# The opening stage of a DiT trunk kernel on one NeuronCore: vectors spread by diagonal tiles, paired squares, five parts of modulation rows between the products, and three tile pairs instead of four

## The chip, the core and the metric

The kernel runs on one core of one Trainium2 chip. The core has TensorE (PE in the profile; PEld is its weight load), VectorE (DVE), ScalarE (ACT), GpSimd (POOL) and SyncE (SP), which issues most of the DMA transfers. The metric is device time in microseconds (us) for one execution; lower is better.

## The reference, cut to what matters

The model is two layers over 256 latent tokens and 256 context tokens of width 1024, all in float32. Every sub-layer starts with an RMS norm whose gain and shift come from a modulation vector, and the first sub-layer is a half-step SwiGLU:

```python
silu_c, silu_cc = jax.nn.silu(c), jax.nn.silu(c_ctx)
m  = (silu_c  @ w_mod[0] + b_mod[0])        # 9 vectors of 1024: shift, scale, gate, ...
mc = (silu_cc @ w_mod[0] + b_mod[0])
h  = rms_norm(x, g) * (1 + scale) + shift   # for x with m, for ctx with mc
a, b = jnp.split(h @ w13, 2, axis=-1)       # w13: 1024 x 5632
x  = x + 0.5 * gate * ((jax.nn.silu(a) * b) @ w2)
```

The change touches what happens before and during the first products `h @ w13`: the norm's sum of squares, the first two of the nine modulation vectors (shift and scale of 1024 entries, for both streams), and the first tiles of `h @ w13`.

## The kernel before, in words

Activations lie transposed: `X` holds 8 parts of 128 features by 512 tokens (256 latent, then 256 context). A "part" k is one such block of 128 features, and is also one block of the contraction of `h @ w13`. Nearly every product is made three times with single-pass float32 operands (`mm3`, lines 147 to 150): each operand is split into a rounded high piece and the rest (`split`, lines 152 to 154: a cast on ACT, a subtraction on DVE), and low times high, high times high and high times low are summed in PSUM. Products that go to PE as plain float32 are two instructions each in the trace.

The program's scheduler orders the instructions of each engine by its own estimates, keeping dependencies; `tc.keep_in_program_order` (called `pin`) puts one instruction behind the instruction that was written just before it for the same engine. PSUM has 8 banks, handed out by `bank()`.

The stage to be changed is `start()` (lines 639 to 743). It loads the two vectors (`cT`), spreads silu of them over all partitions with 16 small products against the identity (line 665) into `cc`, squares the 8 parts of `X` on ACT and sums them over partitions with 8 products against `ones` (lines 679 and 680), and turns that into `rb`, the reciprocal root (lines 681 and 685). The modulation of 5 of the 8 parts comes from DVE: `use_mod` (line 80) multiplies a 128 x 1024 block of `w_mod` with `cc` and sums each row, four instructions for a part (shift and scale, two streams). The modulation of the other three parts (`NR = 3`) comes from PE: `by_rows` (lines 691 to 709) multiplies `cT` with rows of `w_mod`, copies the result to SBUF and transposes it back with small products (line 704). `finish_mod` (lines 84 to 101) adds the bias and forms the gain `gs`; it is two small DVE instructions.

Then a loop runs over the parts in `order`. Per part: load a block of weights for the first four tile pairs of `w13` (`get_raw`, line 645), split it, normalise (`xr`, line 721, DVE; then the modulation, line 724, ACT), split the result into `AH` and `AL`, and make the part's products into the eight PSUM banks `pss`. A tile pair is 128 columns of a and of b, so a part has 4 x 2 x 3 = 24 products with 512 columns. `ffn` (called with `started`) finds the first four tile pairs done and goes on with tile pair 4; each later tile pair is 48 such products.

Of the kernel before, what the change touches and what calls it, by code (L numbers as in the profile page):

```python
# [9 lines left out]
F32 = mybir.dt.float32  # L10
F32R = mybir.dt.float32r
# [11 lines left out]
NH = NF // 2  # L23
EPS = 1e-6
NMOD = 72
NR = 3
WINDOWS = (2, 4, 8, 16)
ATTN_SCALE = 0.125

# [6 lines left out]
def trunk(ctx: ExitStack, tc: tile.TileContext, I, out):  # L36
# [47 lines left out]
    def finish_mod(layer, j, n=1, ks=slice(0, NK)):  # L84
# [7 lines left out]
        V.tensor_tensor(out=m, in0=m, in1=b.broadcast_to([P, ns, n, nk]), op=ALU.add)  # L92
        sub, kind = (j + n - 1) // 3, (j + n - 1) % 3
        last = m[:, :, n - 1]
        if kind == 1:
            g0 = C_NG + (layer * 3 + sub) * NK
            g = par[:, g0 + ks.start:g0 + ks.stop].unsqueeze(1).broadcast_to([P, ns, nk])
            V.scalar_tensor_tensor(out=gs[:, st, sub, ks], in0=last, scalar=1.0, in1=g,
                                   op0=ALU.add, op1=ALU.mult)
        if kind == 2:  # L100
            V.tensor_scalar(gate[:, st, sub, ks], last, 1.0 if j == 5 else 0.5, None, ALU.mult)
# [535 lines left out]


    def start():
        ng = 4  # L640
        order = (0, 5, 1, 6, 2, 7, 3, 4)
        with tc.tile_pool(name="start", bufs=1) as sp:
            def get_raw(k):
                raw = sp.tile([P, ng, 2 * P], F32, name="raw4", bufs=2)
# [4 lines left out]
            cT = sp.tile([P, 2, NK], F32, name="cT")  # L649
            nc.sync.dma_start(out=cT, in_=I["cT"])  # L650
            nc.sync.dma_start(out=ident, in_=I["ident"])
            wm = {(0, 0): load_mod(0, 0, nc.sync)}
            for k in range(0, NK, 2):
                nc.sync.dma_start(out=X[:, k:k + 2], in_=I["xc"][:, k:k + 2])
            wm[0, 1] = load_mod(0, 1, nc.sync)
            S.activation(out=cT, in_=cT, func=AF.Silu)

            S.activation(out=rb[:, 0:1], in_=cT[:, 0, 0:1], func=AF.Sqrt, scale=0.0, bias=epsb)

            for st in range(2):  # L660
                for h in range(2):
                    ps = bank()
                    for k4 in range(4):
                        k = 4 * h + k4
                        PE.matmul(ps[:, k4 * P:k4 * P + P], cT[:, st, k:k + 1].broadcast_to([P, P]),  # L665
                                  ident, start=True, stop=True)
                    S.copy(cc[:, st, h * 512:h * 512 + 512], ps)  # L667
            nc.sync.dma_start(out=par, in_=I["par"])
            wn = [wpool.tile([P, 2, 2 * NR * P], F32, name=n, bufs=3 if i > 1 else 2)
                  for i, n in enumerate(("raw", "raw", "whi", "wlo"))]  # L670
            for i in range(4):
                nc.sync.dma_start(out=wn[i], in_=I["w_modr"][:, 2 * i:2 * i + 2])
            raws = {0: get_raw(0)}
            wm.update({(1, h): load_mod(0, 2 + h, nc.sync) for h in range(2)})
            raws[order[1]] = get_raw(order[1])
            ps = bank()
            for k in range(NK):
                sq = tmp.tile([P, 2 * T], F32, name="sq", bufs=2)
                S.activation(out=sq, in_=X[:, k], func=AF.Square)
                PE.matmul(ps, ones, sq, start=k == 0, stop=k == NK - 1)  # L680
            S.activation(out=rb, in_=ps, func=AF.Sqrt, scale=1.0 / D, bias=epsb)
            for h in range(2):
                use_mod(0, h, wm[0, h])
            finish_mod(0, 0, 2, slice(0, 1))
            V.reciprocal(rb, rb)
            sh = sp.tile([P, NK, ng - 2, 2 * P], F32R, name="sh")
            sl = sp.tile([P, NK, ng - 2, 2 * P], F32R, name="sl")
            wh, wl = ([wpool.tile([P, NK, 2 * P], F32R, name=n, bufs=3) for _ in range(2)]
                      for n in ("whi", "wlo"))

            def by_rows():

                row = sp.tile([2, 2 * NR * P], F32, name="row")
                ps = [bank() for _ in range(2)]
                for k in range(NK):
                    for j in range(2):
                        PE.matmul(ps[j][0:2, :NR * P], cT[:, :, k],  # L697
                                  wn[k // 2][:, k % 2, j * NR * P:(j + 1) * NR * P],
                                  start=k == 0, stop=k == NK - 1)
                for j in range(2):  # L700
                    S.copy(row[:, j * NR * P:(j + 1) * NR * P], ps[j][0:2, :NR * P])
                ps = bank()
                for i in range(2 * NR):
                    PE.matmul(ps[:, 2 * i:2 * i + 2], row[:, i * P:i * P + P], ident[0:2, 0:2],
                              start=True, stop=True)
                for st in range(2):
                    V.tensor_copy(mod[:, st, :16].rearrange("p (j k) -> p j k", j=2)[:, :, NK - NR:],
                                  ps[:, 0:4 * NR].rearrange("p (j k s) -> p s j k", j=2, k=NR)[:, st])
                finish_mod(0, 0, 2, slice(NK - NR, NK))

            by_rows()
            pss = [[bank(), bank()] for _ in range(ng)]
            nxt = 1
            for i, k in enumerate(order):
                raw = raws.get(k) or get_raw(k)
                split(sh[:, k], sl[:, k], raw[:, :2])
                split(wh[0][:, k], wl[0][:, k], raw[:, 2])
                split(wh[1][:, k], wl[1][:, k], raw[:, 3])
                xr = tmp.tile([P, 2 * T], F32, name="sa", bufs=2)
                h = tmp.tile([P, 2 * T], F32, name="h32", bufs=2)  # L720
                V.tensor_tensor(out=xr, in0=X[:, k], in1=rb, op=ALU.mult)
                for st in range(2):
                    ts = slice(st * T, st * T + T)
                    S.activation(out=h[:, ts], in_=xr[:, ts], func=AF.Identity,
                                 scale=gs[:, st, 0, k:k + 1], bias=mod[:, st, k:k + 1])
                if nxt < NK - NR and i in (0, 2, 4, 5):
                    for j in range(2):
                        use_mod(0, 2 * nxt + j, wm.get((nxt, j)) or
                                load_mod(0, 2 * nxt + j, nc.sync), tc.keep_in_program_order)
                    finish_mod(0, 0, 2, slice(nxt, nxt + 1))  # L730
                    nxt += 1
                split(AH[:, k, :2 * T], AL[:, k, :2 * T], h)

                def products(f, k, first, last):
                    for ab in range(2):
                        cs = slice(ab * P, ab * P + P)
                        w = (sh[:, k, f, cs], sl[:, k, f, cs]) if f < 2 else \
                            (wh[f - 2][:, k, cs], wl[f - 2][:, k, cs])
                        mm3(pss[f][ab], *w, AH[:, k, :2 * T], AL[:, k, :2 * T], first, last)

                for f in range(ng):
                    products(f, k, i == 0, i == NK - 1)
        return pss


# [14 lines left out]
def _pack(x, c, ctx, c_ctx, w_mod, b_mod, norm_g, ffn_w13, ffn_w2, w_in_a, qk_norm_g, pool_w,  # L760
# [5 lines left out]
    r["cT"] = ac(np.stack([c[0], c_ctx]).reshape(2, NK, P).transpose(2, 0, 1))  # L766
    r["w_modr"] = ac(w_mod[0][:, :2 * D].reshape(NK, P, 2, NK, P)[:, :, :, NK - NR:]
                     .transpose(1, 0, 2, 3, 4)).reshape(P, NK, 2 * NR * P)
# [70 lines left out]
```

## Time and profile before

| | |
|---|---|
| three runs, median (lowest to highest) | 1141.87 us (1141.83 to 1142.08) |
| the profiled execution | 1142.17 us, of which 1140.4 us are its span |
| TensorE's granted clock, mean | 1.000 |
| HBM read | 240.44 MB, 212 GB/s over the span |
| DVE / ACT busy, share of the span | 76% / 46% |

The span runs from the first to the last instruction. The page lists each engine's busy time, the chain of work that ended last, and groups of instructions by source line; the trace can be asked for any stretch. Matmuls are pipelined, so the duration of one includes its way through the array; what a stream of them costs is the distance from one start to the next (the pitch).

### The profile page before, as it was taken

What the parts mean: (1) busy time and instruction counts of PE and PEld (TensorE: products, weight loads), DVE (VectorE), ACT (ScalarE), POOL (GpSimd) and SP (SyncE); (2) the same over time, 40 slices, a digit from 0 to 9 for tenths busy, and PEclk for the clock granted to TensorE, in tenths of its full rate; (3) what the DMA queues carried; (4) which work ended last, traced back from release to release, by engine and by line L of the source; (5) the groups of instructions that cost most, each with busy time, mean ns of one, the idle gap of its engine ahead of it and who ended that gap; (6) DMA issues with size and microseconds to landing.
All of it is one profiled execution on the core that took longest, in us unless ns stands there. A gap on an engine that the chain in (4) does not pass through costs nothing.

```text
span 1140.4 us, 19165 instructions
## 1 busy us (share of the span) xinstructions
PE 1132.2 (99%) x7696; PEld 1033.9 (91%) x7696; DVE 863.6 (76%) x1582; ACT 522.0 (46%) x816; POOL 68.4 (6%) x140
## 2 busy tenths in 40 slices
PE   8999999999999999999999999999999999999998
PEld 4888888888888897899999999999999899999998
DVE  5967787878789979777778887656667788756663
ACT  5552212223223357664335456435445866434442
POOL 0000111122222200000000000000000000000000
PEclk9999999999999999999999999999999999999999
DMA  8844656788888850556687566456447536546543
GB/s 323 310 148 156 197 186 234 279 282 325 294 297 306 305 196 11 222 172 223 212 305 264 187 219 218 161 167 219 174 143 257 185 114 219 176 154 237 178 143 114
DMA packets 52408, 242.72 MB, mean 213 GB/s; under 512 B 5600, under 2 KB 11488, under 8 KB 38880
## 3 DMA queue, kind: packets, MB, share of 16 engines
q1 hardware_dynamic: 33888, 174.39, 43.4%
q0 software_dynamic: 18432, 67.12, 17.4%
q8 instruction: 60, 0.98, 0.4%
q14 instruction: 28, 0.23, 0.1%
HBM read 240.44 MB, written 1.05 MB: 212 GB/s over the span
## 4 chain that ended last, share of the span: by engine, by line
PE 97%; DVE 1%; ACT 1%; DMA 1%; issue 0%; SPq 0%; DVEq 0%; ACTq 0%
PE ps L148 30%; PE ps L149 30%; PE ps L150 30%; PE ps L697 1%; PE ps L618 1%; PE ps L619 1%; PE ps L617 1%; PE ps L680 1%; PE ps L665 1%; DMA raw<-in_w_out_a 0%; ACT whi L153 0%; PE ps L501 0%; PE ps L469 0%; DVE st L473 0%; PE ps L172 0%; ACT pe L477 0%
## 5 line engine op out<-in xcount | busy, mean ns | idle before, releaser
L148 PE MATMUL ps<-AH,wlo 128*128 128x258 f32 (+2 forms) x1664 | 507.1, 305 | 0.3 <-ACT AH L153 0.3
L149 PE MATMUL ps<-AH,whi 128*128 128x258 f32 (+2 forms) x1664 | 506.6, 305 | 0.0
L150 PE MATMUL ps<-AL,whi 128*128 128x258 f32 (+2 forms) x1664 | 505.5, 305 | 0.0
L153 ACT CAST whi<-raw 128x1024 fp32r<-128x1024 f32 (+2 forms) x354 | 313.7, 921 | 363.7 <-PE ps L150 260.3
L154 DVE TENSOR_TENSOR wlo<-raw,whi 128x1024 fp32r<-128x1024 f32 (+2 forms) x354 | 367.6, 1064 | 54.4 <-ACT whi L153 53.4
L148 PEld LDWEIGHTS ps<-AH,wlo 128*128 128x128 f32 x1664 | 316.3, 190 | 16.1 <-issue 1.1
L149 PEld LDWEIGHTS ps<-AH,whi 128*128 128x128 f32 x1664 | 314.3, 189 | 14.7 <-issue 0.5
L150 PEld LDWEIGHTS ps<-AL,whi 128*128 128x128 f32 x1664 | 313.4, 189 | 14.5 <-issue 0.2
L150 PE MATMUL ps<-HL,whi 128*128 128x256 f32 (+1 forms) x704 | 218.0, 310 | 0.0
L149 PE MATMUL ps<-HH,whi 128*128 128x256 f32 (+1 forms) x704 | 218.0, 310 | 0.0
L148 PE MATMUL ps<-HH,wlo 128*128 128x256 f32 (+1 forms) x704 | 218.0, 310 | 0.0
L80 DVE CUSTOM_DVE_ANT_0 wm<-wm,cc 128x1024 f32<-128x1024 f32 x138 | 164.7, 1219 | 6.1 <-DMA wm<-in_w_mod 5.0
L148 PEld LDWEIGHTS ps<-HH,wlo 128*128 128x128 f32 x704 | 132.5, 188 | 7.8
L150 PEld LDWEIGHTS ps<-HL,whi 128*128 128x128 f32 x704 | 132.5, 188 | 7.7
L149 PEld LDWEIGHTS ps<-HH,whi 128*128 128x128 f32 x704 | 132.6, 188 | 7.7
L72 POOL DMA_DIRECT2D wm<-in_w_mod x128 | 67.7, 529 | 546.2 <-DVE mod L80 508.6
L206 ACT ACTIVATE sa<-sa,cb 128x256 f32<-128x256 f32 x66 | 33.6, 510 | 119.7 <-DVE sa L205 116.4
L246 DVE SCALAR_TENSOR_TENSOR X<-ps,gate,X 128x256 f32<-128x256 f32 x64 | 30.9, 482 | 48.0 <-PE ps L150 47.9
L204 DVE COPY cb<-ps 128x1 f32<-128x1 f32 x66 | 10.3, 155 | 72.8 <-PE ps L150 72.7
L212 DVE TENSOR_TENSOR h<-ps,sa 128x512 f32<-128x512 f32 x22 | 15.2, 692 | 43.4 <-PE ps L150 34.2
L80 DVE CUSTOM_DVE_ANT_0 junk<-wm,cc 128x1024 bf16<-128x1024 f32 x34 | 41.4, 1218 | 8.6 <-ACT cc L667 7.2
L154 DVE TENSOR_TENSOR HL<-h,HH 128x256 fp32r<-128x256 f32 (+1 forms) x88 | 42.3, 485 | 0.0
(162 smaller groups left out, 705.3 us busy)
## 6 DMA issues: line engine op xcount, KB each, us to landing
raw<-in_w SPq DMA_DIRECT2D x84, 1024.0 KB, 4.9
wm<-in_w_mod POOLq DMA_DIRECT2D x128, 512.0 KB, 5.0
raw<-in_w SPq DMA_DIRECT2D x64, 704.0 KB, 4.1
wm<-in_w_mod SPq DMA_DIRECT2D x10, 512.0 KB, 6.4
raw<-in_w_in_a SPq DMA_DIRECT2D x5, 1024.0 KB, 7.8
raw<-in_w SPq DMA_DIRECT2D x8, 512.0 KB, 5.3
raw<-in_w_out_a SPq DMA_DIRECT2D x4, 1024.0 KB, 5.0
raw<-in_w_in_cu SPq DMA_DIRECT2D x4, 1024.0 KB, 4.8
```

The lines of the kernel that those rows point to most:

```text
L72: eng.dma_start(out=w, in_=I["w_mod"][layer, i])
L80: pin(V.tensor_tensor_reduce(out=res, in0=w, in1=cc[:, st, :], scale=1.0, scalar=0.0, op0=ALU.mult, op1=ALU.add, accum_out=mod[:, 2 * laye ...
L148: PE.matmul(ps, wl, xh, start=first, stop=False)
L149: PE.matmul(ps, wh, xh, start=False, stop=False)
L150: PE.matmul(ps, wh, xl, start=False, stop=last)
L153: S.copy(hi, src)
L154: pin(V.tensor_tensor(out=lo, in0=src, in1=hi.bitcast(F32), op=ALU.subtract))
L206: S.activation(out=sa[:, :T], in_=sa[:, :T], func=AF.Silu, bias=cb[:, 0:1])
L212: V.tensor_tensor(out=h32[:, :n], in0=ps[1][:, :n], in1=sa[:, :n], op=ALU.mult)
L246: V.scalar_tensor_tensor(out=X[:, m, :T], in0=ps[:, :T], scalar=gate[:, 2 * layer, sub, m:m + 1], in1=X[:, m, :T], op0=ALU.mult, op1=ALU.add)
L617: PE.matmul(ps[b], AL[:, k, ts], hi[:, ws], start=(k == 0), stop=False)
L618: PE.matmul(ps[b], AH[:, k, ts], hi[:, ws], start=False, stop=False)
```

## The change

- `order` is now (3, 4, 0, 5, 1, 6, 2, 7). The modulation of five parts, `ROWS = (3, 4, 5, 6, 7)`, comes from `by_rows`, one part at a time; that of parts 0, 1 and 2 from `use_mod` on DVE, in the loop passes 1, 2 and 4 (`jobs`).
- `by_rows(k)` makes 8 products with 32 columns of weights (`c32`, two vectors padded with zeros) and 256 columns of data, into the four 32-row quarters of one bank in turn, copies the bank to SBUF, and sums the quarters in two small products with a selecting matrix `sel`. Part 3 is done before the loop, part 4 between the halves of part 3's products, and parts 5, 6 and 7 after the first third of the products of the part before.
- `cc` is made by two DVE products of the identity with the vectors (`diag`) and four products with `ones`; the copy to SBUF moves from ACT to DVE.
- The squares of parts 0 to 5 are added in pairs on DVE, so 5 products with `ones` are left of 8.
- `rb` is finished in two halves, latent and context. The first part's products are made in two halves too.
- Four products of `ones` with a piece of `X`, whose result isn't used, stand ahead of the loop.
- Three tile pairs instead of four are made in the opening (`ng = 3`); the fourth is made in `ffn`.
- The loads are put in another order; `raw4` has four buffers.

```diff
+ROWS = (3, 4, 5, 6, 7)
...
-        V.tensor_tensor(out=m, in0=m, in1=b.broadcast_to([P, ns, n, nk]), op=ALU.add)
+        V.tensor_tensor(out=m, in0=m if src is None else src, in1=b.broadcast_to([P, ns, n, nk]),
+                        op=ALU.add)
...
-        ng = 4
-        order = (0, 5, 1, 6, 2, 7, 3, 4)
+        ng = 3
+        order = (3, 4, 0, 5, 1, 6, 2, 7)
+
+        jobs = {1: 0, 2: 1, 4: 2}
...
+            for ks in (slice(0, 2), slice(2, 4), slice(4, 6), slice(6, 7), slice(7, 8)):
+                nc.sync.dma_start(out=X[:, ks], in_=I["xc"][:, ks])
+            nc.sync.dma_start(out=par, in_=I["par"])
+            rows, raws, wm = {}, {}, {}
+            rows[3] = get_rows(3)
+            raws[3] = get_raw(3)
+            rows[4] = get_rows(4)
+            raws[4] = get_raw(4)
+            wm.update({(0, j): load_mod(0, j, nc.sync) for j in range(2)})
+            raws[0] = get_raw(0)
+            rows[5] = get_rows(5, "whi", 3)
+            raws[5] = get_raw(5)
+            wm.update({(1, j): load_mod(0, 2 + j, nc.sync) for j in range(2)})
...
+            diag = cc.rearrange("p s (k c) -> p s k c", k=NK)
+            bc = [bank() for _ in range(4)]
             for st in range(2):
+                V.tensor_tensor(out=diag[:, st], in0=ident.unsqueeze(1).broadcast_to([P, NK, P]),
+                                in1=c32[:, :, st:st + 1].broadcast_to([P, NK, P]), op=ALU.mult)
                 for h in range(2):
-                        PE.matmul(ps[:, k4 * P:k4 * P + P], cT[:, st, k:k + 1].broadcast_to([P, P]),
-                                  ident, start=True, stop=True)
-                    S.copy(cc[:, st, h * 512:h * 512 + 512], ps)
+                    PE.matmul(bc[2 * st + h], ones, diag[:, st, 4 * h:4 * h + 4],
+                              start=True, stop=True)
...
                 S.activation(out=sq, in_=X[:, k], func=AF.Square)
-                PE.matmul(ps, ones, sq, start=k == 0, stop=k == NK - 1)
-            S.activation(out=rb, in_=ps, func=AF.Sqrt, scale=1.0 / D, bias=epsb)
+                if k in (0, 2, 4):
+                    even = sq
+                    continue
+                if k < 6:
+                    V.tensor_tensor(out=sq, in0=even, in1=sq, op=ALU.add)
+                PE.matmul(ps, ones, sq, start=k == 1, stop=k == NK - 1)
+            pin = tc.keep_in_program_order
+            for b in range(4):
+                pin(V.tensor_copy(cc[:, b // 2, b % 2 * 512:b % 2 * 512 + 512], bc[b]))
...
+            def by_rows(k):
+                w = rows.pop(k)
+                for kt in range(NK):
+                    g = kt % 4
+                    pin(PE.matmul(rw[32 * g:32 * g + 32, :2 * P], c32[:, kt], w[:, kt],
+                                  start=kt < 4, stop=kt >= 4))
+                row = sp.tile([P, 2 * P], F32, name="row", bufs=2)
+                pin(S.copy(row, rw[:, :2 * P]))
                 for j in range(2):
+                    PE.matmul(rw[:, 2 * P + 2 * j:2 * P + 2 * j + 2], row[:, j * P:j * P + P], sel,
+                              start=True, stop=True)
+                finish_mod(0, 0, 2, slice(k, k + 1),
+                           rw[:, 2 * P:2 * P + 4].rearrange("p (j s) -> p s j", j=2).unsqueeze(3))
...
+            by_rows(order[0])
+            for _ in range(4):
+                pin(PE.matmul(rw[:, :2 * P], ones, X[:, 0, :2 * P], start=True, stop=True))
             for i, k in enumerate(order):
...
+                if i == 0:
+                    for ts in halves:
+                        if ts.start:
+                            pin(V.reciprocal(rb[:, ts], rb[:, ts]))
+                            subs(pin)
+                            rest(halves[0])
+                        pin(V.tensor_tensor(out=xr[:, ts], in0=X[:, k, ts], in1=rb[:, ts],
+                                            op=ALU.mult))
+                        if ts.start == 0:
+                            casts(pin)
+                        normed(ts, AH[:, k, ts])
+                        normed(ts, h[:, ts])
+                    rest(halves[1])
+                else:
+                    casts(pin)
+                    subs(pin)
+                    V.tensor_tensor(out=xr, in0=X[:, k], in1=rb, op=ALU.mult)
+                    for ts in halves:
+                        normed(ts, h[:, ts])
+                    split(AH[:, k, :2 * T], AL[:, k, :2 * T], h)
...
+                if i in jobs:
+                    d = jobs[i]
                     for j in range(2):
+                        use_mod(0, 2 * d + j, wm.pop((d, j)), tc.keep_in_program_order)
+                    finish_mod(0, 0, 2, slice(d, d + 1))
...
+                if i == 0:
+                    for ts in halves:
+                        if ts.start:
+                            by_rows(ahead)
+                        for j, (a, x) in enumerate(((0, AH), (0, AL), (1, AH))):
+                            for f, ab in ws:
+                                PE.matmul(pss[f][ab][:, ts], ws[f, ab][a], x[:, k, ts],
+                                          start=j == 0 and ts.start == 0, stop=False)
+                else:
+                    for f, ab in ws:
+                        if ahead is not None and (f, ab) == (1, 0):
+                            by_rows(ahead)
+                        mm3(pss[f][ab], *ws[f, ab], AH[:, k, :2 * T], AL[:, k, :2 * T], False,
+                            i == NK - 1)
```

Here `casts` and `subs` are the two casts (ACT) and two subtractions (DVE) that split the part's weights, `normed` is the modulation (line 724 before), `rest` the subtraction that gives `AL`, and `ahead` the next part in `order` if it is one of `ROWS`.

More of the change, by code (lines that the diff above doesn't have):

```diff
@@ L647, in get_raw, with get_rows @@
                 return raw
-            cT = sp.tile([P, 2, NK], F32, name="cT")
-            nc.sync.dma_start(out=cT, in_=I["cT"])
-            nc.sync.dma_start(out=ident, in_=I["ident"])
[L652 to L658, printed above, removed]
+            def get_rows(k, home="raw", bufs=2):
+                w = wpool.tile([P, NK, 2 * P], F32, name=home, bufs=bufs)
+                nc.sync.dma_start(out=w, in_=I["w_modr"][ROWS.index(k)])
+                return w
@@ L688, in start @@
[L688 to L699, printed above, removed]
+                if k in (0, 2, 4):
+                    even = sq
+                    continue
@@ new lines, in start @@
+                if k < 6:
[4 more added lines that the diff above has]
+                pin(V.tensor_copy(cc[:, b // 2, b % 2 * 512:b % 2 * 512 + 512], bc[b]))
+            for st in range(2):
+                ts = slice(st * T, st * T + T)
+                S.activation(out=rb[:, ts], in_=ps[:, ts], func=AF.Sqrt, scale=1.0 / D, bias=epsb)
@@ new lines, in start @@
+            rw = bank()
+            halves = [slice(st * T, st * T + T) for st in range(2)]
+            pin(V.reciprocal(rb[:, :T], rb[:, :T]))
+            def by_rows(k):
[6 more added lines that the diff above has]
+                pin(S.copy(row, rw[:, :2 * P]))
@@ L732, in start @@
-                split(AH[:, k, :2 * T], AL[:, k, :2 * T], h)
-                def products(f, k, first, last):
-                    for ab in range(2):
[L736 to L742, printed above, removed]
+                parts = ((sh[:, k], sl[:, k], raw[:, :2]), (wh[:, k], wl[:, k], raw[:, 2]))
@@ new lines, in casts, with subs, normed @@
+                def casts(pin=lambda ins: ins):
+                    for w, l, r in parts:
+                        pin(S.copy(w, r))
+                def subs(pin=lambda ins: ins):
+                    for w, l, r in parts:
+                        pin(V.tensor_tensor(out=l, in0=r, in1=w.bitcast(F32), op=ALU.subtract))
+                def normed(ts, out):
+                    st = ts.start // T
+                    S.activation(out=out, in_=xr[:, ts], func=AF.Identity,
+                                 scale=gs[:, st, 0, k:k + 1], bias=mod[:, st, k:k + 1])
```

84 lines of the change are left out of this document (38 added, 46 removed).

## The prediction

> **What bounds the kernel now.** The page comes first: busy shares, then the chain that ended last.
>
> ```profile
> span 1140.4 us, 19165 instructions
> PE 1132.2 (99%) x7696; PEld 1033.9 (91%) x7696; DVE 863.6 (76%) x1582; ACT 522.0 (46%) x816; POOL 68.4 (6%) x140
> PE 97%; DVE 1%; ACT 1%; DMA 1%; issue 0%; SPq 0%; DVEq 0%; ACTq 0%
> ```
>
> PE is busy for all but 8.2 us, and 97% of the chain is PE. So the kernel ends when PE's queue has been worked off: whatever moves the moment at which the opening's products are done moves the end by as much, and nothing later takes it up. The chain over the first 30 us shows what PE does ahead of them (start, length, line), and the timeline shows the product stream.
>
> ```profile
> 3.31 6.15 PE ps L665 x32
> 9.46 7.26 PE ps L680 x16
> 16.72 10.41 PE ps L697 x32
> 27.13 0.76 PE ps L704 x6
> 28.78 0.76 PE ps L704 x6
> 29.53 0.43 PE ps L148
> 70.08 0.39 PE L149 MATMUL ps<-AH,sh 128*128 128x512 f32 x1
> 81.88 0.39 PE L149 MATMUL ps<-AH,whi 128*128 128x512 f32 x1
> 68.66 0.60 ACT L211 ACTIVATE sa<-ps 128x512 f32<-128x512 f32 x1 [4.03 <-PE ps L150]
> ```
>
> The two L149 rows are 51 products apart: 11.80 / 51 = 0.2314 us for a product of 512 columns without a break. ScalarE's row marks the end of the first tile (three products) of the last part: its last product started a product's length (0.39) before 68.6, and the next 21 follow at 0.2314, so the 192 opening products (8 parts x 24) are off PE's queue at 73.3. They alone cost 192 x 0.2314 = 44.4. So **28.9 us of the opening is not products**, and the chain shows it gap-free: 6.15 spreading vectors, 7.26 squares, 10.41 rows, some 2 transposes, and 3.3 for the first loads.
>
> The other engines, by windows (PE, PEld, DVE, ACT busy in each):
>
> ```profile
> 0.00:5.00 5.00, 1.69 (x8) 1.72 (x9) 0.22 (x2) 3.08 (x4) 0.20 (x4) 1.00 0.50 158
> 5.00:10.00 5.00, 5.00 (x28) 4.69 (x28) 1.23 (x2) 3.29 (x6) 0.00 (x0) 1.00 0.97 356
> 30.00:35.00 5.00, 5.00 (x23) 4.05 (x22) 5.00 (x14) 3.22 (x8) 0.00 (x0) 1.00 0.60 212
> 65.00:70.00 5.00, 5.00 (x23) 4.10 (x22) 0.62 (x2) 0.60 (x1) 0.00 (x0) 1.00 0.62 210
> ```
>
> From 30 us DVE is as full as PE, and only at 65 is it ahead. Its work is hidden because a part has 24 products (5.6 us). With three tile pairs a part has 18 x 0.2314 = 4.17 us of cover.
>
> **The change, part by part.** After the change 144 products lie in the opening and 48 are tile pair 3, done at once behind it, so the same 44.4 us of products end at: start S of the first product + 44.4 + other PE work behind S + PE's gaps behind S. That is set against 73.3.
>
> *Spreading and squares.*
>
> ```profile
> 2.67 0.22 ACT L656 ACTIVATE cT<-cT 128x16 f32<-128x16 f32 x1 [0.65 <-DMA cT<-in_cT]
> L665 PE MATMUL ps<-ident,cT x6: 421/421/421, 5.8 to 6.9; 128*128 128x128 f32 x6
> L665 PE MATMUL ps<-ident,cT x7: 274/275/275, 8.3 to 9.0; 128*128 128x128 f32 x7
> L679 ACT ACTIVATE sq<-X 128x512 f32<-128x512 f32 x8 | 4.9, 628 | 2.3 <-PE ps L680 1.7 <-DMA X<-in_xc 0.6
> L163 DVE TENSOR_TENSOR acc<-acc,sq 128x512 f32<-128x512 f32 x7 | 4.8, 685 | 0.0
> L667 ACT COPY cc<-ps 128x512 f32<-128x512 f32 x4 | 2.3, 581 | 1.6 <-PE ps L665 1.6
> 45.17 1.22 DVE L80 CUSTOM_DVE_ANT_0 junk<-wm,cc 128x1024 bf16<-128x1024 f32 x1
> 46.92 1.22 DVE L80 CUSTOM_DVE_ANT_0 wm<-wm,cc 128x1024 f32<-128x1024 f32 x1
> 48.06 1.22 DVE L80 CUSTOM_DVE_ANT_0 junk<-wm,cc 128x1024 bf16<-128x1024 f32 x1
> ```
>
> The silu ends at 2.9. The diagonal product (128 x 1024 on DVE) isn't in the trace; between one 512-column add (0.69) and two (1.37) I take the 1.22 of the like-sized L80: the two halves are ready at 4.4 and 5.6. The four spreads are eight 512-column instructions; L680's pitch is 7.26 / 16 = 0.454. But PE's first 4.5 us run at half speed although the granted clock reads 1.00: L665's starts are 0.22 apart at 5.8 to 6.9 and 0.117 at 8.3 to 9.0. So 4.4 to 8.9 gives 4.9 instructions at 0.91 and the other 3.1 take 1.4: 10.3 us, against 9.46 now. Nothing is gained; the wide products only do in one piece what 32 short ones did.
>
> The five square products then stand in a chain, because `sq` has two buffers: the second square of a pair (0.63) waits for the product that reads its buffer, the add (0.69) follows, and then the product (0.91): 2.23 per pair. First product 10.3 to 11.2 (its inputs are there by 7.5), then 13.4, 15.65, and the last single one 0.63 + 0.91 later: 17.2, against 16.72 now. If spreads and squares ran without cold clock and waits, 18 x 0.454 from 4.4 would end at 12.6: that is the low end of this term, 4.6 less. The four copies of `cc` (0.58 on ACT, L667) move to DVE behind the last add (14.7) and are through by 17.2, ahead of the root.
>
> *Part 3's modulation.* It is pinned behind the last square product.
>
> ```profile
> 448.81 1.73 PE L501 MATMUL ps<-pt,VV 128*64 128x256 f32 x13 [0.37 <-ACT pt L493]
> 442.09 0.59 PE L450 MATMUL ps<-pd,poolw 128*128 128x256 f32 x2
> 27.06 0.82 PE L704 MATMUL ps<-ident,row 2*128 2x2 f32 x6
> L504 ACT COPY hn<-ps 128x256 f32<-128x256 f32 x4 | 1.5, 382 | 1.3 <-PE ps L377 1.3
> 15.27 0.17 DVE L92 TENSOR_TENSOR mod<-mod,par 128x4 f32<-128x4 f32 x1
> 15.47 0.16 DVE L98 SCALAR_TENSOR_TENSOR gs<-mod,par 128x2 f32<-128x2 f32 x1
> L174 DVE RECIPROCAL rb<-rb 128x256 f32<-128x256 f32 x4 | 7.0, 1754 | 2.2 <-ACT rb L173 2.2
> L173 ACT ACTIVATE rb<-ps,epsb 128x256 f32<-128x256 f32 x4 | 1.9, 476 | 1.3 <-PE ps L172 1.2
> L192 DVE TENSOR_TENSOR hn<-X,rb 128x256 f32<-128x256 f32 x8 | 3.0, 418 | 0.0
> L724 ACT ACTIVATE h<-sa,mod,gs 128x256 f32<-128x256 f32 x16 | 8.9, 595 | 9.4 <-DVE sa L721 6.8 <-DVE gs L98 2.4
> L153 ACT CAST AH<-h 128x512 fp32r<-128x512 f32 x8 | 5.0, 620 | 0.2
> ```
>
> The eight products are 16 instructions of 256 columns. Untiled ones stand 0.59 - 0.38 = 0.21 apart (L450); those with 64-column tiles, alternating between two, (1.73 - 0.38) / 12 = 0.1125 (L501). Four tiles in turn could reach half of that again, 0.056, if they really run four abreast. But each float32 product is two instructions for the same tile, and if the second waits for the first and all start in order, only neighbours overlap: 0.1125. I take that, the nearest row: 1.8 us; ends 0.9 and 3.4. [...]
>
> So: rows 17.2 to 19.0, copy 0.38, four transposes 3 x 0.115 + 0.25 = 0.6 (L704's pitch and length), gain 0.4, the half norm 0.42 (pinned behind the gain), modulation 0.60: **S = 21.4**. Root and half reciprocal (0.48 + 1.75 from 17.2) are done at 19.4, hidden; so are the loads: 2.2 MB of X and vectors plus 1.05 MB of rows and par lie ahead, and the windows have moved 2.6 MB by 10 us and 356 GB/s after. Later loads are further ahead still: the issues that SP gains stand behind transfers needed after 21, and POOL's loads of `w_mod` only follow freed buffers. The four idle products (1.7 us) fill the wait for DVE and are hidden.
>
> *The parts*, each from the start of its products; a gap is idle PE.
>
> ```profile
> L154 DVE TENSOR_TENSOR sl<-raw,sh 128x512 fp32r<-128x512 f32 x8 | 5.5, 685 | 0.0
> L154 DVE TENSOR_TENSOR wlo<-raw,whi 128x256 fp32r<-128x256 f32 x16 | 6.3, 418 | 0.0
> L721 DVE TENSOR_TENSOR sa<-X,rb 128x512 f32<-128x512 f32 x8 | 5.4, 686 | 0.6 <-ACT h L724 0.6
> ```
>
> Part 3: 6 products of half width (6 x 0.116 = 0.7), then `AL` is needed, but DVE has pinned ahead of it the second reciprocal (1.75), two subtractions (0.69 + 0.42) and then `rest` (0.42): a gap of 2.0. Twelve more (1.4), rows of part 4 (1.8), second half with transposes (2.6): S + 8.5. Part 4's `AH` comes 3.5 after its rows (0.38 + 0.6 + 0.4, two modulations 1.19, cast 0.62, hand-overs 0.3): S + 9.4, a gap of 0.9.
>
> Part 4 to part 0: part 0 gets its gain from `use_mod`, and the first of these is pinned behind the subtraction that gives part 4's `AL`. Two in a row start 1.14 apart (46.92, 48.06). From part 4's `AH`: 0.69 + 4.6 + gain 0.4 + modulation 1.1 + cast 0.62 = 7.4, against 4.17 of products: **a gap of 3.2**.
>
> Part 0 to part 5: products, rows and transposes take 4.17 + 1.8 + 0.46 = 6.4. DVE has four `use_mod` again; the gain of part 5 is ready 4.2 into it, just as the fourth starts (4.1). Behind that one the next `AH` is at 7.8, ahead of it at 6.4; the rows of 45 to 48 us show that the order does put other work between two L80. I take the middle: 0.7. Part 1 to part 6 is the same: 0.7. Parts 5 and 6 have no such work (0.69 `AL`, 1.1 subtractions, 0.69 norm, 1.1 modulation and 0.62 cast are 4.2, against 4.17): 0. Part 2 to part 7: the gain comes 6.7 in, against 6.4: 0.3.
>
> **Sum:** 21.4 + 44.4 + four times (1.8 + 0.46) = 9.0 + gaps 2.0 + 0.9 + 3.2 + 0.7 + 0.7 + 0.3 = 7.8, together 82.6. Against 73.3 that is 9.3 later. The profiled execution took 1142.17, 0.3 above the median shown; so 1142.17 + 9.3 = 1151.5, and by the median 1151.2. PE's work itself shrinks by only some 2.5 us, while an opening without gaps gets some 14 us in which PE waits.
>
> **Rivals.**
>
> *Four tiles abreast*: rows take 0.9. That is 0.9 less in S, part 3 and part 2, and 0.6 less in parts 0 and 1, where DVE then bounds: 3.9 less, 1147.3. For it: L501's tiles do overlap. Against: the pairs. With the low end of the squares' term as well, 1143.
>
> *PE stays the bound* (the other side): the order fills every gap, as it does now. PE's own work is 4.4 + 5.9 + 4.5 + 2.3 + 1.7 idle products + 44.4 + 9.0 = 72.2: 1140.8, no change; with four abreast, five times 0.9 less: 1136.3, faster. It decides once gaps and chains cost under some 3 us. For it: 99% busy now. Against: the pins, which put `use_mod` behind `AL`.
>
> *The clock falls back* in a gap: PE's opening shows half speed for 4.5 us, so each such gap costs 2.2 more: 1153.4, or 1155.6 for two. [...] The gap of 3.2 is the longest in the sum.
>
> *No overlap at all*, so that the change doesn't do what it says: rows take 3.4, five times 1.6 more: 1159.2.
>
> **How the numbers follow.** Forecast 0.52, four abreast 0.20, PE stays the bound 0.13, clock 0.10, no overlap 0.05. A measurement of this kernel tells about 0.2% (2.3 us) from no change. Faster by more: 0.09, from PE staying the bound with four abreast. Within: 0.04 from the same rival with pairs, and 0.05 from four abreast with early squares: 0.09. Slower: the rest, 0.82. The range reaches from four abreast with early squares (1143) to two cold gaps and a little more (1157), and leaves out 0.18.
>
> **What would show it.** The first `AH` product near 21 us; the last square product near 17; rows' starts 0.11 apart (0.06 for four abreast, 0.21 for none); a PE gap of some 3 us ahead of the second part after part 3, ended by ScalarE's cast, with four L80 on DVE before it; tile pair 3 done near 82.6. I would be wrong if the squares are through by 13, if L80 runs ahead of part 4's `AL`, or if loads come last anywhere.

## The result, and the profile after

| | before | after |
|---|---|---|
| median of 4 runs (lowest to highest) | 1141.97 us (1141.83 to 1142.39) | 1155.14 us (1154.33 to 1156.58) |
| profiled execution, and its span | 1142.17 us, 1140.4 us | 1154.33 us, 1152.6 us |
| granted TensorE clock, mean | 1.000 | 0.997 |

The changed kernel is slower: ratio 1.0116, 95% interval 1.0099 to 1.0134. That is 13.2 us by the medians and 12.2 us between the two profiled executions, where 9.3 us had been forecast. First the page: span, busy shares and the chain that ended last.

```profile
span 1152.6 us, 19270 instructions
PE 1131.5 (98%) x7748; PEld 1033.1 (90%) x7748; DVE 863.7 (75%) x1575; ACT 520.4 (45%) x811; POOL 68.4 (6%) x140
PE 93%; DVE 3%; ACT 2%; DMA 1%; issue 0%; DVEq 0%; ACTq 0%
```

TensorE has almost the same work as before (1131.5 us against 1132.2), but there are now 21.1 us of the span in which it does nothing, against 8.2. The chain says the same: PE lost 4 points, and DVE (1% to 3%) and ACT (1% to 2%) gained. Where does it end? The same ScalarE instruction of tile pair 4 (the silu, line 211 before, 213 after) in the two timelines:

```profile
79.12 0.60 ACT L211 ACTIVATE sa<-ps 128x512 f32<-128x512 f32 x1 [0.83 <-PE ps L150]
```

```profile
91.41 0.60 ACT L213 ACTIVATE sa<-ps 128x512 f32<-128x512 f32 x1 [3.10 <-PE ps L152]
```

It comes 12.3 us later, and the span is 12.2 us longer. So everything happens in the opening, and nothing later gives any of it back. Now PE's timeline of the changed kernel (start, length, line, count; in brackets the idle time before it and what ended it):

```profile
10.53 1.02 PE L699 MATMUL ps<-sq,ones 128*128 128x512 f32 x2
12.99 1.12 PE L699 MATMUL ps<-sq,ones 128*128 128x512 f32 x2 [1.44 <-DVE sq L698]
15.56 4.46 PE L699 MATMUL ps<-sq,ones 128*128 128x512 f32 x6 [1.45 <-DVE sq L698]
19.96 1.07 PE L716 MATMUL ps<-raw,c 128*32 128x256 f32 x16
21.52 0.61 PE L721 MATMUL ps<-cs,row 128*128 128x2 f32 x4 [0.49 <-ACT row L719]
22.44 1.99 PE L733 MATMUL ps<-X,ones 128*128 128x256 f32 x8 [0.31 <-DVE mod L93]
24.08 0.82 PE L810 MATMUL ps<-AH,sh 128*128 128x256 f32 x4
25.84 0.74 PE L810 MATMUL ps<-AL,sh 128*128 128x256 f32 x4 [0.70 <-DVE AL L755]
31.92 0.50 PE L150 MATMUL ps<-AH,sl 128*128 128x512 f32 x1 [0.56 <-ACT AH L155]
39.65 0.79 PE L150 MATMUL ps<-AH,sl 128*128 128x512 f32 x1 [3.30 <-ACT AH L155]
48.73 0.50 PE L150 MATMUL ps<-AH,sl 128*128 128x512 f32 x1 [1.64 <-ACT AH L155]
```

The first three rows are the chain of the squares: a product, then 1.44 us in which PE waits for DVE's add. The last three are the starts of parts 4, 0 and 5, each after a wait for ScalarE's cast. Line 716, the rows, takes 1.07 us for 16 instructions; line 733 is the four products whose result isn't used. And the `x6` at 15.56 takes 4.46 us, where six such instructions at 0.454 would take 2.7. The windows show why (last columns: granted clock, DMA share, GB/s):

```profile
10.00:15.00 5.00, 2.68 (x6) 0.68 (x4) 0.87 (x2) 1.89 (x3) 0.00 (x0) 1.00 1.02 414
15.00:20.00 5.00, 4.43 (x10) 1.70 (x13) 2.90 (x5) 1.26 (x2) 0.00 (x0) 0.66 1.03 384
35.00:40.00 5.00, 1.70 (x7) 1.11 (x7) 4.68 (x11) 1.71 (x3) 0.00 (x0) 0.93 0.86 287
40.00:45.00 5.00, 5.00 (x30) 3.17 (x30) 3.84 (x7) 1.20 (x3) 0.66 (x1) 0.72 0.91 299
```

Twice PE was idle for a large part of a window (2.32 and 3.30 us of 5), and in the next one the granted clock fell (0.66 and 0.72 in the mean of 5 us; before, every window of the opening read 1.00).

### The profile page after: what moved, and what is told of

Its sections match the earlier page's. It is cut to its first block, busy times and chain, and to the rows that moved or that the text cites. A ratio compares the mean times of both kernels' runs of the same rounds, so it can differ in the third digit from the quotient of the medians.

```text
span 1152.6 us, 19270 instructions
## 1 busy us (share of the span) xinstructions
PE 1131.5 (98%) x7748; PEld 1033.1 (90%) x7748; DVE 863.7 (75%) x1575; ACT 520.4 (45%) x811; POOL 68.4 (6%) x140
## 4 chain that ended last, share of the span: by engine, by line
PE 93%; DVE 3%; ACT 2%; DMA 1%; issue 0%; DVEq 0%; ACTq 0%
PE ps L150 29%; PE ps L152 29%; PE ps L151 29%; PE ps L620 1%; PE ps L621 1%; PE ps L619 1%; PE ps L699 1%; DMA raw<-in_w 1%; ACT whi L155 1%; ACT h L751 0%; PE ps L688 0%; DMA raw<-in_w_out_a 0%; PE ps L503 0%; PE ps L471 0%; DVE st L475 0%
## 5 line engine op out<-in xcount | busy, mean ns | idle before, releaser
L155 ACT CAST whi<-raw 128x1024 fp32r<-128x1024 f32 (+1 forms) x340 | 310.3, 946 | 375.0 <-PE ps L152 278.2
L156 DVE TENSOR_TENSOR wlo<-raw,whi 128x1024 fp32r<-128x1024 f32 (+1 forms) x340 | 363.9, 1096 | 59.9 <-ACT whi L155 58.3
L81 DVE CUSTOM_DVE_ANT_0 wm<-wm,cc 128x1024 f32<-128x1024 f32 x134 | 160.1, 1220 | 5.0 <-DMA wm<-in_w_mod 4.3
L155 ACT CAST HH<-h 128x256 fp32r<-128x256 f32 (+1 forms) x88 | 39.7, 454 | 1.1 <-DVE h L210 1.0
```

Of the source, the lines that this page charges most:

```text
L81: pin(V.tensor_tensor_reduce(out=res, in0=w, in1=cc[:, st, :], scale=1.0, scalar=0.0, op0=ALU.mult, op1=ALU.add, accum_out=mod[:, 2 * laye ...
L155: S.copy(hi, src)
L156: pin(V.tensor_tensor(out=lo, in0=src, in1=hi.bitcast(F32), op=ALU.subtract))
```

## The experiments

Eight kernels were run. Times are medians; each ratio is to the kernel before, run beside it.

**1. The chain of the squares** (`e1_buffers`): the squares get more buffers, so that none waits for a product.

```diff
-                sq = tmp.tile([P, 2 * T], F32, name="sq", bufs=2)
+                sq = tmp.tile([P, 2 * T], F32, name="sa" if k > 5 else ("sq", "h32")[k % 2], bufs=2)
```

> The changed kernel, with the squares put into other buffers: even parts in the two of sq, odd ones in the two of h32, the last two in those of sa. My theory: the squares wait in a chain for their two buffers (product, square, add, product), which ends at 19.95 us. Freed of it, the ten instructions stand behind the spreads at 0.43 us each from 10.1, so the last ends near 14.5, the first part's products start near 18.6 instead of 24.1, and the time falls by about 5.5 us, to 1149.6. Rival, the loads or DVE's work bound the parts that follow: the first product starts earlier and the time falls by 2 us at most.

Measured: 1151.30 us, ratio 1.0083 [1.0068, 1.0098]; 3.8 us less than the changed kernel, between the 5.5 of the theory and the 2 of its rival. PE's timeline:

```profile
13.78 1.88 PE L699 MATMUL ps<-sa,ones 128*128 128x512 f32 x4
15.59 1.07 PE L716 MATMUL ps<-raw,c 128*32 128x256 f32 x16
19.72 0.83 PE L810 MATMUL ps<-AH,sh 128*128 128x256 f32 x4
35.87 0.79 PE L150 MATMUL ps<-AH,sl 128*128 128x512 f32 x1 [3.27 <-ACT AH L155]
```

The rows start at 15.59 instead of 19.96 and the first product at 19.72 instead of 24.08: 4.4 us of the opening are the squares' two buffers and what they do to the clock, which stays at 1.00 here until 35.7. The gap of 3.3 us ahead of part 0, with its slow products behind it, is untouched. Of the 4.4 us, 0.6 are lost again at once: part 3 now waits 1.30 us for `AL`, where the changed kernel waits 0.70.

**2. Parts with `use_mod` two places later** (`e2_order`).

```diff
-        order = (3, 4, 0, 5, 1, 6, 2, 7)
-        jobs = {1: 0, 2: 1, 4: 2}
+        order = (3, 4, 5, 0, 6, 1, 7, 2)
+        jobs = {1: 0, 3: 1, 5: 2}
```

> The changed kernel with order (3, 4, 5, 0, 6, 1, 7, 2) and use_mod in passes 1, 3 and 5: the four use_mod for part 0 now have a whole part between them and their use. My theory: the gap of 3.45 us before part 0 and the half clock behind it (1.5 us) go, a gap near 1.8 us like that before part 5 now comes in their place: 3 us less, 1152. Rival, DVE's work as a whole bounds the opening with three tile pairs: the same work in another order, within 0.7 us of the changed kernel.

Measured: 1148.43 us, ratio 1.0058 [1.0043, 1.0073]: 6.7 us less by the medians, 5.0 between the profiled executions. That is more than the 3 expected. PE's waits behind part 3:

```profile
32.40 0.50 PE L150 MATMUL ps<-AH,sl 128*128 128x512 f32 x1 [0.56 <-ACT AH L155]
40.31 0.50 PE L150 MATMUL ps<-AH,sl 128*128 128x512 f32 x1 [1.80 <-ACT AH L155]
51.02 0.50 PE L150 MATMUL ps<-AH,sl 128*128 128x512 f32 x1 [0.46 <-ACT AH L155]
```

No wait is longer than 1.80 us any more, and no window behind 20 us reads under 1.00. The four `use_mod` no longer hold back the part right behind them. The expectation had priced that wait and its slow clock. It had not priced that the later waits shrink too: 1.64, 0.27 and 0.71 us in the changed kernel, the last of them for a row copy (below), against 0.46 here. That the medians differ by more than the profiled executions goes with the clock: it falls once in the profiled one, behind the squares (between 16 and 20 us), where its mean is 0.998, and in the other three executions the mean is 0.999 or 1.000.

**3. Is it the clock?** (`e3_fill`): five products without a use are put into the gap ahead of part 0; DVE's work is left as it is.

```diff
+                    for _ in range(5 if i == 1 else 0):
+                        pin(PE.matmul(rw[:, :2 * P], ones, X[:, 0, :2 * P], start=True, stop=True))
```

> The changed kernel with five idle float32 products (256 columns, about 2.1 us, result unused) pinned behind part 4's products, in the gap before part 0. Rival clock: the granted clock halves because PE idles for 3.4 us; filled, it stays at 1.00, the products of part 0 stand 0.23 apart from the start, and 1.5 us are saved: 1153.6. If the clock has nothing to do with the idle time, it halves all the same and the time stays within 0.5 us of the changed kernel.

Measured: 1154.57 us, ratio 1.0113 [1.0096, 1.0130], 0.6 us less than the changed kernel, within the spread of either.

```profile
40.11 0.50 PE L150 MATMUL ps<-AH,sl 128*128 128x512 f32 x1 [1.14 <-ACT AH L155]
48.02 0.50 PE L150 MATMUL ps<-AH,sl 128*128 128x512 f32 x1 [1.81 <-ACT AH L155]
```

The window from 40 to 45 reads 1.00 instead of 0.72, so the mechanism is right. But part 5 starts only 0.7 us earlier than in the changed kernel (1.2, if counted from the start of part 4, which is 0.5 later in this execution), and behind a wait of 1.81 us: its `AH` comes when DVE is done with the next four `use_mod`, whatever PE's clock was. So of the slow products' cost 1.2 us at most came back.

**4. Both repairs and an early silu table** (`e4_three`): experiments 1 and 2, and a silu of a constant at the very start, so that ScalarE loads its table (1.28 us, from 2.60 on in the changed kernel) before the vectors are there.

```diff
+            S.activation(out=rb[:, 1:2], in_=epsb, func=AF.Silu)
```

> The changed kernel with the buffers and the order of the two experiments before, and a silu of a constant ahead of the first load's arrival, so that ScalarE's table is loaded by then (its load starts at 2.60 us in the changed kernel, at 0.73 before). My theory, waits in series: 5.5 + 3 + 1 us less, 1145.6, still behind the kernel before. Rival, one resource bounds the opening (loads, or DVE's work): less than 6 us less, over 1149.

Measured: 1146.45 us, ratio 1.0039 [1.0024, 1.0054]: 8.7 us of the 13.2 are undone. The mean granted clock is 1.000.

```profile
36.21 0.50 PE L150 MATMUL ps<-AH,sl 128*128 128x512 f32 x1 [1.80 <-ACT AH L155]
```

This is the longest wait that is left. The first product comes at 19.9, no earlier than in experiment 1: the early table gave nothing. The spreads start earlier (4.6 instead of 5.2 there), but the squares then wait for the loads of `X`, 2.5 us in three waits of ScalarE, the longest 1.1. Some 4.3 us remain against the kernel before.

**5. The shorter rows alone** (`e5_cols`): the kernel before, with its three parts' rows made in four 32-column tiles and summed by `sel`.

```diff
-                        PE.matmul(ps[j][0:2, :NR * P], cT[:, :, k],
+                        g = 32 * (k % 4)
+                        PE.matmul(ps[j][g:g + 32, :NR * P], c32[:, k],
...
-                                  start=k == 0, stop=k == NK - 1)
+                                  start=k < 4, stop=k >= 4)
...
-                    PE.matmul(ps[:, 2 * i:2 * i + 2], row[:, i * P:i * P + P], ident[0:2, 0:2],
+                    PE.matmul(ps[:, 2 * i:2 * i + 2], row[:, i * P:i * P + P], sel,
```

> The kernel before with one part of the change alone: the rows of its three parts as products in four column tiles (all rows ahead of the loop as now, four tile pairs, its own order). My theory, the change loses by its waits and not by its products: PE's rows fall from 10.4 us to about 3, the loads of the rows (the last lands at 20.5 us) and DVE then hold the start, and 3 to 5 us are saved: 1137 to 1139, faster than both. [...]

Measured: 1142.10 us, ratio 1.0003 [0.9994, 1.0013]: no change, where 1137 to 1139 had been expected. A miss, and it tells most.

```profile
20.93 1.49 PE L703 MATMUL ps<-wlo,c 128*32 128x384 f32 x8 [0.42 <-DMA wlo<-in_w_modr]
23.64 1.50 PE L710 MATMUL ps<-sel,row 128*128 128x2 f32 x12 [1.21 <-ACT row L707]
26.57 0.47 PE L148 MATMUL ps<-AH,sl 128*128 128x512 f32 x1 [1.43 <-DVE sl L154]
25.00:30.00 5.00, 3.57 (x12) 2.82 (x12) 4.75 (x13) 2.94 (x7) 0.00 (x0) 0.77 0.36 119
30.00:35.00 5.00, 5.00 (x21) 4.04 (x20) 5.00 (x13) 2.47 (x6) 0.00 (x0) 0.89 0.86 315
```

The first three rows are PE's timeline, the last two windows. The rows are now so short that they wait for their own loads (0.42), the transposes for ScalarE (1.21), and the first product for DVE (1.43). It comes at 26.57. In the kernel before, the first was not the one at 29.53 of the chain:

```profile
27.82 0.50 PE L148 MATMUL ps<-AH,sl 128*128 128x512 f32 x1
```

Three products came there, then the last transposes, and the rest from 29.46 on; without that break they would have started at 28.8. So the stream starts 2.2 us earlier. And then the clock falls: 0.77 and 0.89, eight products at 0.43, which takes back 1.6 us. In this execution the silu of tile pair 4 is still 0.7 us early (78.40 against 79.12), with a mean granted clock of 0.999; in seven of the ten executions that mean is 0.997, so most lost more to the clock than this trace shows. The column tiles are not what was dear: the rows take 5.1 us instead of 10.41. But the old rows had covered loads, copies and splits.

**6. Three tile pairs alone** (`e6_three_pairs`): the kernel before with `ng = 3`.

```diff
-        ng = 4
+        ng = 3
```

> The kernel before with one other part alone: three tile pairs in the opening instead of four, the fourth made behind it. Rival DVE: a part then has 4.17 us of products for the same normalising and use_mod work, DVE becomes the bound and 3 to 4 us are lost: 1145.5. My theory gives the number of tile pairs less weight, the kernel before has no use_mod that is needed in the very next part: 0 to 1.5 us lost, 1142 to 1143.5.

Measured: 1147.90 us, ratio 1.0057 [1.0042, 1.0072]: 6.1 us slower, against 0 to 1.5 by the theory and 3 to 4 by its rival. One of three waits of PE, and the windows around it:

```profile
59.61 0.49 PE L148 MATMUL ps<-AH,sl 128*128 128x512 f32 x1 [2.28 <-ACT AH L153]
55.00:60.00 5.00, 2.72 (x12) 1.78 (x11) 5.00 (x13) 4.03 (x8) 0.53 (x1) 1.00 0.66 201
60.00:65.00 5.00, 5.00 (x17) 3.92 (x16) 5.00 (x6) 2.45 (x4) 0.00 (x0) 0.66 0.33 103
```

DVE is busy for every bit of both windows, and PE waits (0.69, 0.36 and 2.28 us in the three places): with 18 products to a part, DVE is the bound. These 3.3 us are what the rival had. And behind the longest wait the clock falls once more (0.66), which adds up to 1.7 us: half of the 3.4 us at 0.50. Some 1 us stays unexplained. (This execution is the slowest of the four; its first load landed late, and its spreads start at 4.9 instead of 3.31.)

**7. Without the idle products** (`e7_no_idle`): the changed kernel less the four products ahead of the loop.

```diff
-            for _ in range(4):
-                pin(PE.matmul(rw[:, :2 * P], ones, X[:, 0, :2 * P], start=True, stop=True))
```

> The changed kernel without the four idle products ahead of the loop. They run from 22.44 to 24.06 us while the first part's high piece is ready at 23.55, so I expect the first product 0.5 us earlier and the time 0.5 us less, 1154.6. Rival: they keep the clock up; without them PE idles from 22.1 to 23.6 and the products after it run at half clock for a while: 1 us or more lost, 1156.

Measured: 1157.56 us, ratio 1.0141 [1.0126, 1.0157], 2.4 us slower than the changed kernel. My theory had 0.5 us to win; the rival with the clock was right.

```profile
23.92 0.75 PE L808 MATMUL ps<-AH,sh 128*128 128x256 f32 x4 [1.48 <-ACT AH L749]
26.16 1.08 PE L808 MATMUL ps<-AL,sh 128*128 128x256 f32 x4 [1.26 <-DVE AL L753]
22.95:26.36 3.41, 1.18 (x7) 0.98 (x8) 3.41 (x7) 1.09 (x2) 0.00 (x0) 1.00 1.02 383
26.36:29.77 3.41, 3.41 (x24) 2.73 (x27) 1.71 (x4) 1.09 (x2) 0.00 (x0) 0.50 0.84 304
```

The first product comes 0.16 us earlier (23.92), but PE is busy for only 1.18 us of the 3.41 us from 22.95, and for the next 3.41 us the clock is exactly 0.50. The clock falls twice more in this execution, at 50.2 and 74.1, and not at the gap ahead of part 0, where it falls in the changed kernel. So the idle products stand for one of these falls, and the 2.4 us are the sum of all.

**8. Experiment 5 with its idle stretches filled** (`e8_cols_filled`).

```diff
+                for _ in range(3):
+                    pin(PE.matmul(idle, ones, X[:, 0, :2 * P], start=True, stop=True))
...
+                for _ in range(4):
+                    pin(PE.matmul(idle, ones, X[:, 0, :2 * P], start=True, stop=True))
```

> e5_cols (the kernel before with its three parts' rows as column-tiled products, and everything else as it was) came out level with the kernel before, 1142.10 against 1141.79. Its trace has two idle stretches of PE behind the rows (1.21 us, then 1.43 us) and after them eight or nine products 0.43 us apart at a granted clock of 0.50. This kernel is e5_cols with idle float32 products in those two stretches (three behind the rows, four behind the transposes, some 0.4 us each); nothing else differs. Theory clock (the half clock after the idle stretches took most of what the shorter rows gave): the granted clock stays at 1.00 between 25 and 32 us, the first products are 0.23 apart, 1.5 to 1.9 us come back: 1140.2 to 1140.6. Rival DVE (from 25 to 62 us DVE is 95 to 100% busy in e5_cols, so PE's regained time becomes a gap later on): the clock stays at 1.00 but gaps of 1 to 2 us in all appear between 30 and 62 us, each ended by DVE or by ScalarE's cast: 1141.5 to 1142.3, no change against e5_cols.

Measured: 1141.31 us, ratio 0.9994 [0.9985, 1.0003]; 0.8 us under experiment 5, and not to be told from the kernel before. It lies between the two theories, and the trace has some of each:

```profile
25.00:30.00 5.00, 5.00 (x24) 4.14 (x23) 5.00 (x10) 3.03 (x7) 0.00 (x0) 1.00 0.53 176
40.00:45.00 5.00, 4.61 (x20) 3.46 (x19) 5.00 (x13) 3.78 (x8) 0.00 (x0) 1.00 0.82 276
60.00:65.00 5.00, 4.29 (x19) 3.30 (x18) 4.25 (x6) 3.82 (x6) 0.00 (x0) 1.00 0.06 22
```

The clock stays at 1.00 and PE is full from 25 to 30. But then PE waits 0.39 us at 43 and 0.71 us at 60, both times for ScalarE's cast behind a busy DVE (5.00 of 5 us from 40 to 45, 4.71 from 55 to 60). Against experiment 5 the front wins 2.2 us, 0.6 by an earlier first product (25.96) and 1.6 by the clock, and half of it turns up in these two waits. So in the kernel before, DVE stands right behind PE in the opening: the rows' three runs of products take 5.1 us in all instead of 10.41, and less than 1 us of that was had. A kernel that is clearly faster than both was not found. The three pairs could not be undone in the changed kernel by themselves: four pairs fill all 8 buffers that `bank()` hands out (the kernel's pool `pp`), and `rw` needs a ninth. That was not tried in another form either.

## Why the prediction was right, and where it was not

The forecast had PE's last opening product at 82.6; it was at 85.55 (the 54 products from 73.06 on stand 0.2314 apart). Against the sum:

| term | forecast | measured |
|---|---|---|
| first product S | 21.4 | 24.08 |
| 192 products | 44.4 | 44.4 |
| rows and transposes behind S, four times | 9.0 | 6.6 |
| gaps behind S (measured: what is left, slow clock included) | 7.8 | 10.4 |
| end | 82.6 | 85.5 |

**S is the term that was mis-sized**, by 2.7 us. The mechanism was the one predicted, a chain of squares, add and product through two buffers. Its links were a little longer: products start 2.46 and 2.57 us apart where 2.23 had been worked out, some 0.6 us with both. The largest part, 1.7 us, is a thing that the step left out: while PE waits in this chain it is busy for 2.68 us of 5, and then the clock falls and the last six instructions take 4.46 us instead of 2.7. The step's words "the last single one 0.63 + 0.91 later: 17.2" assumed the full clock, and they count one single product where two are left (parts 6 and 7), another 0.3; the squares were through at 20.0. Experiment 1 takes chain and clock away together and S falls by 4.4 us. What stands between the squares and S came out right, 4.1 against 4.2, by two errors: the rows took 0.7 us less, but then half the reciprocal (1.75 us from 20.57) and the idle products were last. These were priced as hidden, and in the place they have they hold the first product back by about 0.5 us (`AH` was ready at 23.55). Experiment 7 shows that this is cheap.

The silu came 1.2 us late, since its table load stood behind the wait for the vectors, from 2.60 on. The first square product was late by only 0.2 us, and that is luck: the spreads started 1.0 us later than forecast (5.42 against 4.4), but PE's slow first stretch was shorter than the 4.5 us assumed (the spreads' instructions start 0.86 us apart up to 8.15 and 0.43 apart from 8.81 on, so some 3.2 us), and they took 5.1 us instead of 5.9. Experiment 4 shows no gain from an early table.

**The rows** run four abreast: (1.07 - 0.38) / 15 = 0.046 us from start to start, where the forecast took 0.1125 from tiles in pairs, and had 0.056 as the rival. Rows and transposes together add 1.65 us to a part instead of 2.26 (by the starts of the products around them in part 1). Against the untiled pitch that the prediction read, the four tiles give 0.21 / 0.046 = 4.6 times. By the starts of the products around them the rows alone add 1.09 us in part 1, or 0.068 us for each instruction, and then it is 3.1 times. But the rival's sum failed: 1147.3 left the other terms as they were, and the 2.4 us won behind S were lost in the gaps. That these two errors, 2.4 and 2.6 us, nearly cancel in the sum is luck too.

**The gap behind part 4** was placed and priced right: 3.30 us of idle PE against 3.2, ended by ScalarE's cast (3.6 if counted by the starts of the products, as in the table). DVE's timeline has the cause, the pinned order:

```profile
31.90 0.69 DVE L156 TENSOR_TENSOR AL<-h,AH 128x512 fp32r<-128x512 f32 x1
32.51 1.22 DVE L81 CUSTOM_DVE_ANT_0 junk<-wm,cc 128x1024 bf16<-128x1024 f32 x1
36.18 1.22 DVE L81 CUSTOM_DVE_ANT_0 wm<-wm,cc 128x1024 f32<-128x1024 f32 x1
```

Four `use_mod` stand from 32.51 to 37.4 behind part 4's `AL`, and only then come gain, modulation and cast. Experiment 2 moves them out of the way.

**The other gaps**: part 3 to part 4 cost 2.0 instead of 2.9. Part 0 to part 5 cost 3.3 instead of 0.7: 1.64 of waiting, and the rest PE's slow clock, which had a rival's place with a chance of 0.10. Experiment 3 shows that this clock is real and worth 1.2 us there at most, as DVE would have been late anyway. By the number alone, the measured 1155.14 lies nearest to that rival's 1155.6 for two slow stretches, and the clock did fall twice. But a fall costs some 1.7 us (half of the 3.42 us at 0.50 that each of these two lasted), not 2.2, and the first came in the chain of the squares, where the rival had not looked. The step that failed between parts 0 and 5 is the middle that I took for DVE's order (the gain between ahead of and behind the fourth `use_mod`); it was behind it. Part 1 to part 6 shows only 0.4 us (forecast 0.7), and that because the scheduler had put six of tile pair 3's products ahead of it.

**Loads** were said to come last nowhere. In one place one did:

```profile
66.94 1.99 ACT L155 CAST whi<-raw 128x1024 fp32r<-128x1024 f32 x2 [4.38 <-DMA raw<-in_w]
68.84 0.36 ACT L719 COPY row<-ps 128x256 f32<-128x256 f32 x1
```

ScalarE waits 4.38 us for tile pair 4's weights, and the copy of part 7's rows stands behind these two casts; PE stands idle for 0.71 us because of it, where 0.3 had been forecast for another reason.

**Why it is slower at all.** The forecast's reason was that the change takes little from PE and opens waits. Experiments 5, 6 and 8 show it from the other side. Shorter rows alone win nothing, because loads, ScalarE and DVE come right behind PE; three tile pairs alone lose 6.1 us, because DVE's work per part no longer fits behind 18 products. With the squares' chain and the `use_mod` order mended, 4.3 us are left (experiment 4), and the three tile pairs are the likely reason. Taking them out of that kernel was not tried, so this last share is argued, not shown.

## What to carry to other kernels

When the bounding engine is full only because its work covers that of the others, making that work shorter buys nothing: look first at which engine stands second, and by how much (here DVE: with 5.3 us less of rows, less than 1 us was had). A DVE job for a later part that is pinned ahead of what the next part needs can cost most of its length (here 3.3 of 4.9 us, and the slow clock behind it); in the new order the longest wait was 1.8. In a chain of products and squares that share buffers, count the buffers before the instructions.

## What the runs showed of the hardware

The clock's falls were the surprise: they came not only behind one long gap, but also behind several short waits in one stretch. The slow stretches are of one length. Worked out from the mean clock of windows of 1 us (in the changed kernel 0.72 from 15 to 16 and 0.57 from 18 to 19, which puts the slow stretch from 15.44 to 18.86), nine of them in seven kernels lasted 3.40 to 3.42 us each. These are windows of 3.41 us: the three that end at a fall in the changed kernel (first two) and in experiment 6, and one of experiment 7:

```profile
12.03:15.44 3.41, 1.12 (x2) 0.30 (x2) 1.31 (x3) 1.45 (x3) 0.00 (x0) 1.00 1.03 410
35.93:39.34 3.41, 0.42 (x2) 0.00 (x0) 3.09 (x9) 1.45 (x3) 0.00 (x0) 1.00 0.79 238
```

```profile
57.11:60.52 3.41, 1.13 (x5) 0.78 (x5) 3.41 (x8) 3.28 (x6) 0.48 (x1) 1.00 0.54 165
```

```profile
36.60:40.01 3.41, 1.60 (x7) 0.96 (x6) 3.31 (x9) 0.32 (x1) 0.00 (x0) 1.00 0.87 318
```

Behind the first three, with 0.42 to 1.13 us of busy PE, the granted clock was 0.50 for about 3.4 us; behind the fourth, with 1.60, it stayed at 1.00, although PE had a gap of 3.29 us there (38.20 to 41.49), as long as the one of 3.30 us that came ahead of the fall in the changed kernel. So the length of a gap alone does not tell: this one was followed by no fall, and two waits of 1.44 and 1.45 us in one window were. The falls of one execution, in the two that had more than one, lie multiples of 3.41 us apart: 15.44 and 39.34 are 23.90 us (7 x 3.41) apart, and in experiment 7 16.12 and 26.36 are 10.24 us (3 x 3.41) apart. The two later falls in experiment 7, at 50.2 and 74.1, are 7 x 3.41 apart as well. The window at 36.60 starts 3 x 3.41 behind the fall at 26.36. Why the falls lie so, and why the clock stayed up in that gap, was not shown.

Busy time alone draws no line, though. In experiment 7 the clock fell behind 1.60 us of busy PE too (46.84 to 50.25, with a wait of 1.81 us) and behind 1.89 (70.73 to 74.14), and in experiment 5 behind 1.98, of which 0.9 were transposes of two columns. A product counts as busy for 0.39 us, but stands 0.2314 us from the next. Counted by 0.2314 for each product started, the two windows of 1.60 hold some 1.45 us (the clock stayed) and some 1.3 us (it fell), by an estimate from the timeline. A limit between these would fit both; it was not tested, and how much narrow products count was not measured. The changed kernel also spreads more from run to run (2.25 us, against 0.56 before), and its longest run has the lowest mean clock (0.996, against 0.997 in the other three). The reason was not looked for.
